# A feed-forward product from seven block products instead of eight, in a two-layer streaming encoder

## The chip, the cores and the metric

The kernel runs on one core of one Trainium2 chip, as one program. The metric is the device time of one execution in microseconds (us); 2145.57 us is the median of three runs before the change (2144.13 to 2145.99). The engines are TensorE (PE, with its weight loads as PEld), VectorE (DVE), ScalarE (ACT), GpSimd (POOL) and SyncE (SP), which issues most DMAs. Each works through its own instructions in order and waits on semaphores for the others.

## The reference

Two layers, each a mixer of three kinds of attention and a feed-forward net with a short convolution. 32 sample rows and 512 prompt rows pass together as T = 544 columns. The change lies in the feed-forward net:

```python
def rmsnorm(x, g):
    xf = x.astype(jnp.float32)
    y = xf * lax.rsqrt(jnp.mean(xf * xf, axis=-1, keepdims=True) + EPS)
    return (y * g.astype(jnp.float32)).astype(x.dtype)

def ffn_layer(x, conv_past, w):
    h = rmsnorm(x, w['ffn_norm_g'])
    a, u = jnp.split(h @ w['ffn_w_up'], 2, axis=-1)
    B, S, _ = a.shape
    pad = jnp.zeros((B, CONV_W - 1, D_FF), a.dtype) if conv_past is None else conv_past
    ap = jnp.concatenate([pad, a], axis=1)
    cw = w['ffn_conv_w']
    c = ap[:, 0:S] * cw[0]
    for k in range(1, CONV_W):
        c = c + ap[:, k:k + S] * cw[k]
    c = c + w['ffn_conv_b']
    out = (jax.nn.silu(c) * u) @ w['ffn_w_down']
    return out, ap[:, -(CONV_W - 1):]
```

D_MODEL is 1024 and D_FF 2816, so `h @ ffn_w_up` has 22 column tiles of 128 for `a` and 22 for `u`.

## The kernel before

Everything is kept transposed: a tile has 128 features on the partitions and the 544 rows of x along the free axis, cut into two halves of H2 = 272 for the PSUM banks. Products are made in a split format: each operand is a high part (rounded to fp32r by ACT, line 345) and a low part (the rest, subtracted by DVE, line 355), and `PASSES` multiplies high by high, high by low and low by high, three matmuls for each block of 128 x 128 weights and 272 columns.

Weights come in the order of `plan()`. `Stream.loader` (212) issues one DMA for each column tile into a `ws` buffer; `Stream.splitter` (226) makes its high and low part in two halves of 512 columns, in a `wx` buffer. In the feed-forward stage a pair i is the tile `("a", l, i)` and the tile `("u", l, i)`, each with 8 blocks along the contraction: 2 x 8 x 2 halves x 3 passes = 96 matmuls. The inputs `h` are x times the gain, not yet divided by the root mean square; the factor `rstd` is multiplied in when a bank is read out (861, 862, 866, and `evac`, 568). `norm_tile` (477) makes the `h` tiles after the output product, `norm_rows` (504) makes `rstd` from the sum of squares with two ACT functions, and `rstd` is ready a few us after the first pair has begun on PE.

`up_tasks` (1850) reads `a` out into `ap`, with two old columns before each request group, applies the three-tap convolution on DVE (1874, 1876, 1878: one TENSOR_SCALAR, two SCALAR_TENSOR_TENSOR) and Silu on ACT (1881), multiplies with `u` (1889, 1890) and splits the result into an `act` tile. The order is pairs 0 to 11, then `down_tasks` over the first 11 `act` tiles, pairs 12 to 21, and `down_tasks` over the rest.

The order of instructions on every engine is written by a planner inside the program: `Sched` (113) runs one generator for each piece of work, keeps a due time for each engine with a cost for each operation (line 297: 1.04 ns a column and 75 ns for a DVE sum, 301: 2.4 ns and 270 ns for a POOL sum), takes the piece that is due first, and hands out buffers through `take` and `give` by the counts in `SLOTS` (251). The costs set the order alone; on the chip each engine then follows its list.

Of the kernel before, what the change touches and what calls it, by code (L numbers as in the profile page):

```python
# [10 lines left out]
F32R = mybir.dt.float32r  # L11
# [93 lines left out]
SWG = 18  # L105

# [92 lines left out]
class Stream:  # L199


    RAW = ("kpsb", "vpsb", "kpdf", "vpdf", "ckN", "ckT", "krp", "ukv")
# [23 lines left out]
    def splitter(self):  # L226
        s, K = self.s, self.K
        for key, n in self.plan:
            if key[0] in self.RAW:
                continue  # L230
            yield from s.take("wx")
            yield from s.need(self.raw, key)
            raw = self.raw.pop(key)[0]
            w = K.t(self.pool, [128, 2, 1024], "wx", F32R)
            h = n // 2
            for a in (0, h):
                yield from K.split(w[:, :, a:a + h], raw[:, a:a + h])
            s.give("ws")
            s.put(self.parts, key, w)

# [12 lines left out]
    ws=3, wx=2, h=8, tf=5, tr=2, rstd=1, post=5,  # L253
    u=2, kk=2, vst=2, vn=2, pk=2, b8=2, p1=1, p2=1, p3=2, p4=2, w1=4, w2=2, wk=3, oa=2, qbd=2, n2=1, an=1, os=1, nm=12,
    ckv=1, uk=1, uv=2, qp=1, qr=1, tq=1, E=1, Ke=1, Ko=1,
    x=8, ap=2, cc=2, act=18, sgl=4,
# [3 lines left out]
class Kern:  # L260
# [216 lines left out]
    def norm_tile(self, m, x, gcol, l, R, late=0):  # L477

        g = self.gpl[l][:, gcol + m:gcol + m + 1]
        h = yield from self.al(self.P, [128, 2, T], "h", F32R)  # L480
# [60 lines left out]
    def proj(self, key, R, post, lasth=False, both=False, tag=None):  # L541

        def chunk(k):
            if k == 0:
                w = yield from self.ws.get(*key)
                return w.rearrange("p s (k c) -> p s k c", c=128)

        def wait(k):
            if ("seen", k) not in R:
                yield from self.s.need(R, ("h", k))  # L550
                R["seen", k] = True

# [128 lines left out]
    def qkv_tasks(self, b, l, u, R, dst):  # L681
# [30 lines left out]
        def past():  # L712
# [7 lines left out]
        return [self.proj((c + "k", l, u), R, kpost, False, first), self.proj((c + "v", l, u), R, vpost, False, False, tag),  # L720
                self.proj((c + "q", l, u), R, qpost, False, False, tag), past]
# [9 lines left out]
    def gate_tasks(self, l, n, R):  # L731
        def mk(i):
            def post(box):
                z = yield from self.evac(box, R)
                self.store(self.sig[i], z, "gpsimd" if i >= SWG else "sync")
                self.s.give("tf", 1, 2000.0)
            return self.proj(("g", l, i), R, post, i == 23)
        return [mk(i) for i in gate_ids(n)]

    def br_tasks(self, l):  # L740
# [11 lines left out]
        def mk(m, b):  # L752
            def chunk(k):
                if k == 0:
                    w = yield from self.ws.get("br", l, b, m)
                    return w[:, :, :512].rearrange("p s (k c) -> p s k c", c=128)

            def free(k):
                if m == 7:
                    self.s.give("act" if b == 2 else "h")  # L760
                if k == 3:
                    self.s.give("wx")
# [28 lines left out]
            return lambda: self.gemm(post, 4, lambda w, k, a: w[:, a, k], lambda k, y: self.o[4 * b + k][0][:, y], T, chunk,  # L791
# [651 lines left out]
    def ml_prep(self, l, u, M, d):  # L1443

        def q_task(h):
            def chunk(k):
                if k == 0:
                    if h == 0:
                        w = yield from self.ws.get("uq", l, u)
                        d["uq"] = w[:, :, :512].rearrange("p s (h k c) -> p s h k c", h=2, k=2)  # L1450
                        yield from self.s.need(M, "cq")
                    return d["uq"]

            def free(k):
# [21 lines left out]
            return lambda: self.gemm(post, 2, lambda w, k, a: w[:, a, h, k], lambda k, b: M["cq"][0][:, k, b], T, chunk,  # L1476
# [333 lines left out]
    def out_tasks(self, l, xsrc, X, R):  # L1810
# [9 lines left out]
        def mk(m):  # L1820
            def chunk(k):
                if k == 0:
                    if m == 0:
                        self.s.spawn(loads())
                    w = yield from self.ws.get("out", l, m)
                    return w.rearrange("p s (k c) -> p s k c", c=128)

            def free(k):
                if m == 7:
                    self.s.give("act")  # L1830
                if k == 7:
                    self.s.give("wx")

            def post(box):
# [9 lines left out]
                yield from self.norm_tile(m, x, G_FFN, l, R)  # L1844

            return lambda: self.gemm(post, 8, lambda w, k, a: w[:, a, k], lambda k, b: self.m2[k][0][:, b], T, chunk,
# [3 lines left out]
    def up_tasks(self, l, i, R, acts):  # L1850
# [3 lines left out]
        def apost(box):  # L1854
# [18 lines left out]
            n = T + 2  # L1873
            self.dscale(c, ap[:, 0:n], self.gain(G_CW + i), ALU.mult, self.gain(G_CB + i), ALU.add)
            yield
            self.stt(c, ap[:, 1:n + 1], self.gain(G_CW + NI + i), c, ALU.mult, ALU.add)
            yield
            self.stt(c, ap[:, 2:n + 2], self.gain(G_CW + 2 * NI + i), c, ALU.mult, ALU.add)
            self.s.give("ap")
            yield  # L1880
            self.act(c, c, AF.Silu)
            yield
# [15 lines left out]
        return [self.proj(("a", l, i), R, apost, False, i == 0), self.proj(("u", l, i), R, upost, i == NI - 1, i == 0)]  # L1898

    def down_tasks(self, l, hf, acts, X, fin):  # L1900
        def mk(m):
            def chunk(k):
                if k in (0, 6):
                    w = yield from self.ws.get("dn", l, m, hf, k // 6)
                    return w.rearrange("p s (k c) -> p s k c", c=128)

            def free(k):
                if m == 7:
                    self.s.give("act")
                if k in (5, 10):  # L1910
# [13 lines left out]
            return lambda: self.gemm(post, 11, lambda w, k, a: w[:, a, k % 6], lambda k, b: acts[11 * hf + k][0][:, b], T,  # L1924
# [4 lines left out]
    def run(self):  # L1929
        tc, nc, a, s = self.tc, self.nc, self.a, self.s  # L1930
        with tc.tile_pool(name="P", bufs=1) as P, tc.tile_pool(name="ps", bufs=1, space=PSUM) as ps, \
# [32 lines left out]
            for l in range(L):  # L1964
# [30 lines left out]
                with tc.tile_pool(name="F", bufs=1) as F:  # L1995
# [299 lines left out]
```

## Time and profile before

| | |
|---|---|
| median of the runs | 2145.57 us |
| profiled execution, its own time | 2145.45 us |
| its span | 2143.2 us |
| PE busy | 2090.4 us (98%) |
| DVE busy | 1482.8 us (69%) |
| ACT busy | 1145.4 us (53%) |
| POOL busy | 414.4 us (19%) |
| DMA, mean over the span | 111 GB/s |

The busy time of PE is modelled, since matmuls are pipelined; a stretch of matmuls is better read by its length and their count. A DVE row gives the length of one instruction, but the next one can begin before it ends, so the cost of one in a full queue is the distance from start to start. In the slices of the page PE is at 9 tenths nearly throughout; DVE stands at 6 to 8 tenths in the attention and in the feed-forward product, and falls to 4 in the down product.

### The profile page before, as it was taken

What the parts mean: (1) busy time and instruction counts of PE and PEld (TensorE: products, weight loads), DVE (VectorE), ACT (ScalarE), POOL (GpSimd) and SP (SyncE); (2) the same over time, 40 slices, a digit from 0 to 9 for tenths busy, and PEclk for the clock granted to TensorE, in tenths of its full rate; (3) what the DMA queues carried; (4) which work ended last, traced back from release to release, by engine and by line L of the source; (5) the groups of instructions that cost most, each with busy time, mean ns of one, the idle gap of its engine ahead of it and who ended that gap; (6) DMA issues with size and microseconds to landing.
All of it is one profiled execution on the core that took longest, in us unless ns stands there. A gap on an engine that the chain in (4) does not pass through costs nothing.

```text
span 2143.2 us, 42022 instructions
## 1 busy us (share of the span) xinstructions
PE 2090.4 (98%) x16334; PEld 2041.5 (95%) x16334; DVE 1482.8 (69%) x3217; ACT 1145.4 (53%) x2545; POOL 414.4 (19%) x810
## 2 busy tenths in 40 slices
PE   7999999899999999999989999998999999999999
PEld 7999999899999999999989999998999999999999
DVE  7878798887676664465468777887876766644652
ACT  7867676877444322223367676767764543222321
POOL 2333232334100000000024342323341000000000
PEclk9999999999999999999999999999999999999999
DMA  5333343322562222332433343433226532223222
GB/s 189 106 111 107 129 135 111 107 70 78 197 196 92 89 86 82 99 89 83 127 113 101 106 126 124 145 100 93 84 69 202 185 100 89 83 82 103 82 85 95
DMA packets 86214, 238.44 MB, mean 111 GB/s; under 512 B 10304, under 2 KB 11200, under 8 KB 86016
## 3 DMA queue, kind: packets, MB, share of 16 engines
q1 hardware_dynamic: 82240, 223.51, 32.7%
q0 software_dynamic: 3776, 12.26, 1.6%
q8 instruction: 128, 2.10, 0.4%
q14 instruction: 70, 0.57, 0.1%
HBM read 201.52 MB, written 34.21 MB: 110 GB/s over the span
## 4 chain that ended last, share of the span: by engine, by line
PE 77%; DVE 8%; ACT 8%; issue 3%; POOL 2%; DMA 2%; SPq 0%; ACTq 0%; POOLq 0%; DVEq 0%
PE z L359 54%; PE g L359 19%; PE pv L359 3%; ACT p L289 2%; PE z L365 1%; ACT w L289 1%; ACT tf L289 1%; ACT wx L289 1%; DMA ws<-wts 1%; DVE wx L296 1%; DVE w L296 1%; DVE b L296 1%; DVE tf L296 1%; ACT kk L289 1%; DVE tr L296 0%
## 5 line engine op out<-in xcount | busy, mean ns | idle before, releaser
L359 PE MATMUL g<-h,wx 128*128 128x272 f32 x4800 | 699.8, 292 | 9.1 <-ACT wx L289 9.0
L359 PE MATMUL z<-h,wx 128*128 128x272 f32 x5184 | 655.1, 288 | 5.0 <-DVE x L296 4.8
L359 PEld LDWEIGHTS z<-h,wx 128*128 128x128 f32 x5184 | 652.2, 189 | 6.4 <-DVE x L296 6.3
L359 PEld LDWEIGHTS g<-h,wx 128*128 128x128 f32 x4800 | 641.9, 190 | 16.7 <-ACT wx L289 9.0
L289 ACT ACTIVATE wx<-ws 128x512 fp32r<-128x512 f32 (+3 forms) x656 | 352.3, 561 | 514.7 <-PE z L359 418.1
L296 DVE TENSOR_TENSOR wx<-ws,wx 128x512 fp32r<-128x512 f32 (+3 forms) x656 | 412.8, 634 | 192.5 <-ACT wx L289 190.0
L359 PE MATMUL z<-act,wx 128*128 128x272 f32 x3264 | 410.7, 288 | 0.0
L359 PEld LDWEIGHTS z<-act,wx 128*128 128x128 f32 x3264 | 410.1, 188 | 0.0
L1870 POOL COPY conv<-ap 128x2 f32<-128x2 f32 x44 | 8.2, 185 | 819.8 <-DVE ap L296 819.8
L289 ACT ACTIVATE w<-z 128x512 fp32r<-128x512 f32 (+9 forms) x212 | 90.1, 441 | 76.2 <-PE pv L359 31.5
L296 DVE TENSOR_TENSOR tf<-g,rstd 128x272 f32<-128x272 f32 x184 | 79.7, 433 | 42.0 <-PE g L359 37.5
L296 DVE TENSOR_TENSOR ap<-z,rstd 128x32 f32<-128x32 f32 x132 | 41.2, 341 | 87.5 <-PE z L359 84.2
L296 DVE TENSOR_TENSOR tf<-z,rstd 128x272 f32<-128x272 f32 x96 | 42.1, 438 | 78.0 <-PE z L359 78.0
L289 ACT ACTIVATE cc<-cc 128x546 f32<-128x546 f32 x44 | 29.1, 662 | 119.0 <-DVE cc L304 119.0
L359 PE MATMUL pv<-w,vst 128*128 128x512 f32 (+3 forms) x352 | 82.4, 323 | 3.3 <-DVE w L296 3.0
L289 ACT ACTIVATE p<-p 128x512 f32<-128x512 f32 (+4 forms) x160 | 71.6, 461 | 1.8
L304 DVE SCALAR_TENSOR_TENSOR cc<-ap,gp,cc 128x546 f32<-128x546 f32 x88 | 69.1, 785 | 1.6
L296 DVE TENSOR_TENSOR x<-z,x 128x272 f32<-128x272 f32 x64 | 28.0, 438 | 60.4 <-PE z L359 60.4
L317 POOL TENSOR_SCALAR tr<-tf 128x544 fp32r<-128x544 f32 (+2 forms) x66 | 47.4, 719 | 113.0 <-ACT tf L289 63.7
L296 DVE TENSOR_TENSOR w<-z,w 128x512 fp32r<-128x512 f32 (+5 forms) x124 | 55.9, 465 | 17.3 <-ACT w L289 17.1
L317 POOL TENSOR_SCALAR kk<-kk 64x1024 fp32r<-64x1024 f32 x32 | 42.8, 1338 | 116.2 <-DVE kk L296 114.2
L359 PE MATMUL z<-tr,cr 128*128 128x272 f32 (+2 forms) x264 | 55.6, 302 | 8.8 <-DVE tr L296 5.5
(238 smaller groups left out, 2775.8 us busy)
## 6 DMA issues: line engine op xcount, KB each, us to landing
ws<-wts SPq DMA_DIRECT2D x246, 512.0 KB, 3.5
ws<-wts SPq DMA_DIRECT2D x56, 256.0 KB, 2.9
ws<-wts SPq DMA_DIRECT2D x36, 384.0 KB, 3.1
sgl<-sig SPq DMA_DIRECT2D x46, 272.0 KB, 3.3
ws<-wts SPq DMA_DIRECT2D x32, 320.0 KB, 2.9
sig<-tf SPq DMA_DIRECT2D x36, 272.0 KB, 2.1
tf<-od POOLq DMA_DIRECT2D x24, 272.0 KB, 4.5
od<-oa SPq DMA_DIRECT2D x16, 272.0 KB, 2.2
```

Source lines behind the costliest of these rows:

```text
L289: self.nc.scalar.activation(out=out, in_=in_, func=func, **kw)
L296: self.nc.vector.tensor_tensor(out=out, in0=in0, in1=in1, op=op)
L304: self.nc.vector.scalar_tensor_tensor(out=out, in0=in0, scalar=scalar, in1=in1, op0=op0, op1=op1)
L317: self.nc.gpsimd.tensor_scalar(out=out, in0=in_, scalar1=s1, scalar2=1.0, op0=ALU.mult, op1=ALU.mult)
L359: self.nc.tensor.matmul(out=out, lhsT=lhsT, rhs=rhs, start=start, stop=stop, skip_group_check=not chk)
L365: self.nc.tensor.transpose(out, in_, self.ident[:p, :p])
L1870: nc.gpsimd.tensor_copy(out=cv[:, 0:2], in_=ap[:, 546:548])
```

## The change

For pairs 3 to 21 (`NP = 3`) of each layer the two products are made together. Take the 256 output columns (tile a, tile u), the contraction of 1024 in two halves of 512, and the 544 columns in two halves of 272. This is a product of two 2 x 2 block matrices, eight block products before; Strassen's scheme in Winograd's form makes it from seven products of sums of blocks. On the weight side `Stream.pair` makes S1 = A21 + A22, S2 = S1 - A11, S3 = A11 - A21 and S4 = A12 - S2 on POOL (A11, A12 are the halves of tile a, A21, A22 those of u), and splits seven operands of 512 columns instead of four. They lie alternately in `wx` (now 4 buffers of half the size) and in the new `wy` (3). On the input side `right` makes the normalised tiles with `rstd` and the sums T1 to T4 once a layer, in `h` and `act` buffers, on DVE and POOL, beside pairs 0 to 2, which stay as they were. `strassen` runs the seven products in three PSUM banks a pair, with the products A22 and S4 of one pair between those of the next; ACT copies one bank's state on its way (`shared`), so that sums of products are formed by starting from it or by a DVE addition. The first convolution tap moves from DVE to ACT (`conv_silu`), and as `rstd` is in the inputs, banks are read out without it. The attention loses one `w1` buffer; `ws` goes from 3 to 4 and `sgl` from 4 to 5.

```diff
     def splitter(self):
...
+            if key[0] in "au" and key[2] >= NP:
+                if key[0] == "u":
+                    yield from self.pair(key[1], key[2])
+                continue
...
+    def pair(self, l, i):
+        s, K = self.s, self.K
+        yield from s.need(self.raw, ("a", l, i), ("u", l, i))
+        a, u = self.raw.pop(("a", l, i))[0], self.raw.pop(("u", l, i))[0]
+        src = dict(A11=a[:, :512], A12=a[:, 512:], A21=u[:, :512], A22=u[:, 512:])
...
+        def sums():
+            for n, x, y, op, use in (("S1", "A21", "A22", ALU.add, "u"), ("S3", "A11", "A21", ALU.subtract, "au"),
+                                     ("S2", "S1", "A11", ALU.subtract, ("S1", "a")),
+                                     ("S4", "A12", "S2", ALU.subtract, ("a", "S2"))):
+                src[n] = (yield from K.al(K.F, [128, T], "sgl"))[:, :512]
+                K.ptt(src[n], src[x], src[y], op)
...
+        for j, n in enumerate(("A11", "S1", "S2", "A12", "S3", "A22", "S4")):
+            tag = ("wx", "wy")[j % 2]
...
-    ws=3, wx=2, h=8, tf=5, tr=2, rstd=1, post=5,
+    ws=4, wx=4, h=8, tf=5, tr=2, rstd=1, post=5,
...
+    def conv_silu(self, ap, c, i):
+        n = T + 2
+        self.act(c, ap[:, 0:n], AF.Identity, bias=self.gain(G_CB + i), scale=self.gain(G_CW + i))
+        yield
+        self.stt(c, ap[:, 1:n + 1], self.gain(G_CW + NI + i), c, ALU.mult, ALU.add)
+        yield
+        self.stt(c, ap[:, 2:n + 2], self.gain(G_CW + 2 * NI + i), c, ALU.mult, ALU.add)
...
+    def right(self, l, X, R, Q):
+        s = self.s
+        yield from s.need(R, "rstd")
...
+        def one(k):
+            n = []
+            for m in (k, k + 4):
+                t = yield from self.al(self.F, [128, T], "sgl")
+                self.stt(t, X[m][0], self.gain(G_FFN + m), r, ALU.mult, ALU.mult)
...
+            s.spawn(parts(n2, "sgl", "h", (("B21", k), ("B22", k))))
+            m = yield from self.tf()
+            self.tt(m[:, a], n1[:, b], n1[:, a], ALU.subtract)
+            yield
+            self.ptt(n1[:, b], n2[:, b], n1[:, b], ALU.subtract)
+            yield
+            s.spawn(parts(n1, "sgl", "h", (("B11", k), ("T3", k))))
+            self.tt(m[:, b], n2[:, b], m[:, a], ALU.subtract)
...
+            self.ptt(four["t", k // 2][:, (a, b)[k % 2]], n2[:, a], m[:, b], ALU.subtract)
...
+    def strassen(self, l, ids, Q, acts, last):
...
+        def shared(D):
+            yield from s.need(D, "A11")
+            B = yield from self.al(self.ps, [128, 512], "z")
+            self.copy(B[:, :H2], D["A"][:, :H2])
...
+            self.tt(z[:, H2:], t[:, H2:], D["E"][:, :H2], ALU.add)
...
+        def first(D, i):
...
+            yield from s.need(D, "S4")
+            self.tt(ap[:, 276:548], D["u2"][0][:, :H2], D["E"][:, :H2], ALU.add)
...
+        def go():
+            prev = None
+            for i in ids:
+                D = {}
+                D["A"] = yield from self.al(self.ps, [128, 512], "g")
+                yield from prod(D, i, "A11", "B11", D["A"], True, False)
+                s.spawn(shared(D))
+                s.spawn(first(D, i))
+                if prev:
+                    yield from rest(*prev, 0)
+                D["E"] = yield from self.al(self.ps, [128, 512], "pv")
+                yield from prod(D, i, "S1", "T1", D["E"], True, False)
+                if prev:
+                    yield from rest(*prev, 1)
+                yield from s.need(D, "B")
+                yield from prod(D, i, "S2", "T2", D["B"][0], False, False)
+                yield from prod(D, i, "A12", "B21", D["A"], False, True)
+                yield from s.need(D, "u2")
+                yield from prod(D, i, "S3", "T3", D["B"][0], False, False)
+                prev = (D, i)
...
-                    for i in range(12):
+                    for i in range(NP):
                         lst += self.up_tasks(l, i, R2, acts)
+                    Q = {}
+                    s.spawn(self.right(l, X, R2, Q))
+                    lst.append(self.strassen(l, range(NP, 12), Q, acts, False))
                     lst += self.down_tasks(l, 0, acts, X, None)
-                    for i in range(12, NI):
-                        lst += self.up_tasks(l, i, R2, acts)
-
+                    lst.append(self.strassen(l, range(12, NI), Q, acts, True))
```

What stands in the lists is shown for DVE and POOL in the first block of layer 0. In the rows `wx` and `wy` are split weights, `ws` weights as loaded, `sgl` a sum made by POOL, `z`, `g` and `pv` PSUM banks and `cc` and `ap` tiles of the convolution. Line numbers of the changed kernel are higher by about 50 to 200 than those of the kernel before.

DVE, one pair in the middle of the block, before:

```order
L296 TENSOR_TENSOR wx_10107<-ws_9936,wx_10107 128x512
L313 TENSOR_SCALAR cc_10116<-ap_10077,gp_65 128x546
L304 SCALAR_TENSOR_TENSOR cc_10116<-ap_10077,gp_65,cc_10116 128x546
L296 TENSOR_TENSOR wx_10107<-ws_9936,wx_10107 128x512
L304 SCALAR_TENSOR_TENSOR cc_10116<-ap_10077,gp_65,cc_10116 128x546
L296 TENSOR_TENSOR tf_10144<-z_10103,rstd_8788 128x272
L296 TENSOR_TENSOR tf_10144<-z_10140,rstd_8788 128x272
L296 TENSOR_TENSOR wx_10174<-ws_10014,wx_10174 128x512
L296 TENSOR_TENSOR tf_10144<-tf_10144,cc_10116 128x32
L296 TENSOR_TENSOR tf_10144<-tf_10144,cc_10116 128x512
L296 TENSOR_TENSOR wx_10174<-ws_10014,wx_10174 128x512
L296 TENSOR_TENSOR act_10197<-tf_10144,act_10197 128x544
```

Four weight parts, a read-out with `rstd`, three convolution steps and the gate with its split are the work of a pair.

DVE, one pair in the middle of the block, now:

```order
L347 TENSOR_TENSOR ap_9953<-tf_9961,pv_9968 128x272
L347 TENSOR_TENSOR wx_10149<-ws_9935,wx_10149 128x512
L355 SCALAR_TENSOR_TENSOR cc_10161<-ap_9953,gp_65,cc_10161 128x546
L347 TENSOR_TENSOR wy_10150<-sgl_10151,wy_10150 128x512
L355 SCALAR_TENSOR_TENSOR cc_10161<-ap_9953,gp_65,cc_10161 128x546
L347 TENSOR_TENSOR wy_10192<-ws_9935,wy_10192 128x512
L347 TENSOR_TENSOR tf_10084<-z_9956,cc_10161 128x32
L347 TENSOR_TENSOR tf_10084<-z_9956,cc_10161 128x240
L347 TENSOR_TENSOR wx_10213<-sgl_10174,wx_10213 128x512
L347 TENSOR_TENSOR tf_10084<-tf_10084,cc_10161 128x272
L347 TENSOR_TENSOR tf_10229<-tf_10105,pv_10113 128x272
L347 TENSOR_TENSOR wx_10172<-sgl_10196,wx_10172 128x512
```

The four weight parts have become seven, of which this piece holds five; three of them read a sum made by POOL. The rows that multiplied with `rstd` are gone, and the first convolution tap as well; the additions that read a `pv` bank are new.

POOL, the same place, before (small copies into and out of `ap`, and nothing else in a pair):

```order
L1859 MEMSET ap_9399 128x2
L1870 COPY conv<-ap_9399 128x2
L1871 COPY conv<-ap_9399 128x2
L1858 COPY ap_9537<-gp_65 128x2
L1859 MEMSET ap_9537 128x2
```

No instruction of POOL there has more than two columns.

POOL, the same place, now:

```order
L2054 COPY conv<-ap_9843 128x2
L2055 COPY conv<-ap_9843 128x2
L351 TENSOR_TENSOR sgl_10029<-ws_9850,ws_9875 128x512
L351 TENSOR_TENSOR sgl_10051<-sgl_10006,ws_9850 128x512
L351 TENSOR_TENSOR sgl_10073<-ws_9850,sgl_10051 128x512
L2041 COPY ap_10092<-gp_65 128x2
L2042 MEMSET ap_10092 128x2
L351 TENSOR_TENSOR sgl_10151<-ws_9987 128x512
```

Four sums of 512 columns stand between the small copies, and the first copy into `conv` waits for DVE's `ap`.

## Rows read from the trace of the kernel before

**Rows 1.** the head of the page: span, busy time of each engine, its share and instructions

```profile
span 2143.2 us, 42022 instructions
PE 2090.4 (98%) x16334; PEld 2041.5 (95%) x16334; DVE 1482.8 (69%) x3217; ACT 1145.4 (53%) x2545; POOL 414.4 (19%) x810
```

**Rows 2.** timeline of PE, feed-forward part (start, length, instructions merged, idle before)

```profile
673.11 6.51 PE L359 MATMUL z<-h,wx 128*128 128x272 f32 x51
...
699.82 118.16 PE L359 MATMUL z<-h,wx 128*128 128x272 f32 x942
884.10 120.39 PE L359 MATMUL z<-h,wx 128*128 128x272 f32 x960
...
1952.78 120.39 PE L359 MATMUL z<-h,wx 128*128 128x272 f32 x960
```

**Rows 3.** busy time by stretch: PE, PEld, DVE, ACT, POOL, then clock, DMA

```profile
700.00:818.00 118.00, 118.00 (x944) 118.00 (x944) 74.11 (x146) 34.82 (x58) 9.62 (x40) 1.00 0.27 84
884.00:1004.00 120.00, 120.00 (x961) 120.00 (x960) 74.98 (x148) 35.41 (x59) 9.42 (x38) 1.00 0.29 87
```

**Rows 4.** timeline of DVE in one pair of column tiles, 740 to 750 us

```profile
740.56 0.69 DVE L296 TENSOR_TENSOR wx<-ws,wx 128x512 fp32r<-128x512 f32 x1 [0.27 <-ACT wx L289]
742.47 0.69 DVE L296 TENSOR_TENSOR wx<-ws,wx 128x512 fp32r<-128x512 f32 x1
743.07 0.78 DVE L304 SCALAR_TENSOR_TENSOR cc<-ap,gp,cc 128x546 f32<-128x546 f32 x1
743.77 0.44 DVE L296 TENSOR_TENSOR tf<-z,rstd 128x272 f32<-128x272 f32 x1
747.19 0.79 DVE L296 TENSOR_TENSOR tf<-tf,cc 128x32 f32<-128x32 f32 x2
748.70 0.73 DVE L296 TENSOR_TENSOR act<-tf,act 128x544 fp32r<-128x544 f32 x1
749.34 0.50 DVE L296 TENSOR_TENSOR ap<-z,rstd 128x32 f32<-128x32 f32 x2
```

**Rows 5.** groups by shape, 700 to 818 us; the last row over the whole span

```profile
L313 DVE TENSOR_SCALAR cc<-ap,gp 128x546 f32<-128x546 f32 x10 | 5.6, 562 | 0.0
L289 ACT ACTIVATE wx<-ws 128x512 fp32r<-128x512 f32 x36 | 20.8, 624 | 41.6 <-PE z L359 41.6
L289 ACT ACTIVATE cc<-cc 128x546 f32<-128x546 f32 x10 | 6.6, 662 | 28.2 <-DVE cc L304 28.2
...
L289 ACT ACTIVATE wk<-g 128x272 f32<-128x272 f32 x48 | 18.6, 392 | 2.5 <-PE g L359 1.8
```

**Rows 6.** timelines of POOL and DVE, three places in the attention stage

```profile
218.37 1.29 POOL L300 TENSOR_TENSOR u<-tf,u 64x512 fp32r<-64x512 f32 x1
219.00 0.44 DVE L296 TENSOR_TENSOR tf<-g,rstd 128x272 f32<-128x272 f32 x1 [2.36 <-PE g L359]
219.35 0.68 DVE L296 TENSOR_TENSOR vst<-z,vst 128x512 fp32r<-128x512 f32 x1
...
250.25 3.37 POOL L300 TENSOR_TENSOR u<-tf,u 64x512 fp32r<-64x512 f32 x3 [0.85 <-ACT u L289]
250.28 1.81 DVE L296 TENSOR_TENSOR wx<-ws,wx 128x512 fp32r<-128x512 f32 x1
...
430.74 1.71 POOL L300 TENSOR_TENSOR wk<-wk,tq 64x544 f32<-64x544 f32 x1 [1.24 <-DVE wk L304]
433.11 1.36 POOL L300 TENSOR_TENSOR wk<-wk,tq 64x544 f32<-64x544 f32 x1 [0.66 <-DVE wk L304]
430.51 0.72 DVE L296 TENSOR_TENSOR tr<-tf,tr 128x544 fp32r<-128x544 f32 x1
```

**Rows 7.** groups by shape over the whole span: two-input POOL instructions

```profile
L300 POOL TENSOR_TENSOR p<-p,p 128x256 f32<-128x256 f32 x16 | 13.6, 852 | 17.6 <-DVE b L296 17.5
L300 POOL TENSOR_TENSOR p<-p,p 128x128 f32<-128x128 f32 x16 | 9.2, 577 | 12.7 <-DVE b L296 9.8 <-DVE n L296 2.9
```

**Rows 8.** timeline of ACT after the last norm tile of layer 0

```profile
683.98 0.66 ACT L289 ACTIVATE rstd<-rstd 128x544 f32<-128x544 f32 x1
```

More of the change, by code (lines that the diff above doesn't have):

```diff
@@ L105 @@
 SWG = 18
+NP = 3
 class Fiber:
@@ L238, in splitter @@
+            w = []
+            h = -(-n // 256) * 128
+            for a in range(0, n, h):
+                yield from s.take("wx")
+                if not a:
+                    yield from s.need(self.raw, key)
+                    raw = self.raw.pop(key)[0]
+                m = min(h, n - a)
+                t = K.t(self.pool, [128, 2, 512], "wx", F32R)[:, :, :m]
+                yield from K.split(t, raw[:, a:a + m])
+                w += [t[:, :, c:c + 128] for c in range(0, m, 128)]
             s.give("ws")
@@ L239, in splitter, with used, one @@
             s.put(self.parts, key, w)
+    def pair(self, l, i):
[3 more added lines that the diff above has]
+        src = dict(A11=a[:, :512], A12=a[:, 512:], A21=u[:, :512], A22=u[:, 512:])
+        left = dict(a=5, u=3, S1=2, S2=2, S3=1, S4=1)
+        box = {}
+        def used(*names):
+            for n in names:
+                left[n] -= 1
+                if not left[n]:
+                    s.give("ws" if n in "au" else "sgl")
+        def sums():
[4 more added lines that the diff above has]
+                K.ptt(src[n], src[x], src[y], op)
+                used(*use)
+                s.put(box, n)
+                yield
+        def one(n, t, tag):
+            if n[0] == "S":
+                yield from s.need(box, n)
+            yield from K.split(t, src[n])
+            used(n if n[0] == "S" else "u" if n == "A22" else "a")
+            s.put(self.parts, (n, l, i), ([t[:, :, c:c + 128] for c in range(0, 512, 128)], tag))
+        for j, n in enumerate(("A11", "S1", "S2", "A12", "S3", "A22", "S4")):
+            tag = ("wx", "wy")[j % 2]
+            yield from s.take(tag)
+            if j == 0:
+                s.spawn(sums())
+            t = K.t(K.F if j % 2 else self.pool, [128, 2, 512], tag, F32R)
+            s.spawn(one(n, t, tag))
@@ L1872, in apost @@
             c = yield from self.al(self.F, [128, T + 2], "cc")
[L1873 to L1882, printed above, removed]
+            yield from self.conv_silu(ap, c, i)
             self.s.put(st, "c", c)
@@ L1896, in upost @@
             self.s.put(acts, i, t)
-        return [self.proj(("a", l, i), R, apost, False, i == 0), self.proj(("u", l, i), R, upost, i == NI - 1, i == 0)]
+        return [self.proj(("a", l, i), R, apost, None, i == 0),
+                self.proj(("u", l, i), R, upost, "act" if i == NP - 1 else None, i == 0)]
+    def conv_silu(self, ap, c, i):
[5 more added lines that the diff above has]
+        self.stt(c, ap[:, 2:n + 2], self.gain(G_CW + 2 * NI + i), c, ALU.mult, ALU.add)
+        self.s.give("ap")
+        yield
+        self.act(c, c, AF.Silu)
+        yield
@@ new lines, in right, with parts @@
+    def right(self, l, X, R, Q):
+        s = self.s
+        yield from s.need(R, "rstd")
+        r = R["rstd"][0]
+        a, b = slice(0, H2), slice(H2, T)
+        four = {}
+        def parts(x, src, tag, names):
+            o = yield from self.al(self.P if tag == "h" else self.F, [128, 2, T], tag, F32R)
+            yield from self.split(o, x)
+            s.give(src)
+            for name, c in zip(names, (a, b)):
+                s.put(Q, name, o[:, :, c])
+        def one(k):
[3 more added lines that the diff above has]
+                self.stt(t, X[m][0], self.gain(G_FFN + m), r, ALU.mult, ALU.mult)
+                n.append(t)
+                yield
+            n1, n2 = n
+            s.spawn(parts(n2, "sgl", "h", (("B21", k), ("B22", k))))
+            m = yield from self.tf()
+            self.tt(m[:, a], n1[:, b], n1[:, a], ALU.subtract)
+            yield
+            self.ptt(n1[:, b], n2[:, b], n1[:, b], ALU.subtract)
+            yield
+            s.spawn(parts(n1, "sgl", "h", (("B11", k), ("T3", k))))
+            self.tt(m[:, b], n2[:, b], m[:, a], ALU.subtract)
+            yield
+            if k % 2 == 0:
+                four["t", k // 2] = yield from self.tf()
+            while ("t", k // 2) not in four:
+                yield WAIT
+            self.ptt(four["t", k // 2][:, (a, b)[k % 2]], n2[:, a], m[:, b], ALU.subtract)
+            yield
+            s.spawn(parts(m, "tf", "act", (("T1", k), ("T2", k))))
+            self.count(four, k // 2)
+            if four["n", k // 2] == 2:
+                s.spawn(parts(four["t", k // 2], "tf", "act", (("T4", k - k % 2), ("T4", k - k % 2 + 1))))
+        yield from self.launch([one(k) for k in range(4)], 2)
```

137 lines of the change are left out of this document (99 added, 38 removed).

## The prediction

> **What bounds the kernel now.** I read the head of the page first: PE is busy 2090.4 of 2143.2 us [rows 1], so whatever is saved has to be saved on PE or lost by making PE wait. Then the timeline of PE: the feed-forward product of layer 0 is one block from 673.11 to 699.82 + 118.16 = 818.0 us (pairs 0 to 11) and, after half of the down product, one from 884.10 for 120.39 us (pairs 12 to 21); none of these rows names a wait, and layer 1 repeats the second block to the hundredth [rows 2]. A pair of column tiles is 96 matmuls, and 960 matmuls take 120.39 us: 125.4 ns each, 12.04 us a pair. The granted clock there is 1.00, its upper level, while DVE is busy for 74 of 118 us, ACT for 35 and POOL for 10 [rows 3]. So PE alone bounds this stage, and DVE is the nearest follower.
>
> **What the change takes off PE.** A pair in the new form is 7 products of 4 x 3 = 12 matmuls of the same 272 columns: 84, or 10.53 us. It applies to 19 pairs in each layer: 2 x 19 x 12 x 0.1254 = 57.2 us. That is the ceiling, and it is reached only if the other engines keep a pace of 10.53 us a pair.
>
> **What it puts on DVE.** By the order of instructions a steady period is 15 DVE rows. Spacings from start to start are read off one pair of before [rows 4]: a low part 128x512 takes 0.60 us (742.47 to 743.07), a convolution step 0.70 (743.07 to 743.77), the 544-wide low part 0.64 (748.70 to 749.34); a 272-wide piece takes 0.35 (219.00 to 219.35 in [rows 6]), the 32- and 240-wide ones together 0.42 (0.50 less an overlap of 0.08). Per pair: 7 x 0.60 + 2 x 0.70 + 0.64 + 0.35 = 6.59 us of work whose two inputs both lie in SBUF, and 2 x 0.35 + 0.42 = 1.12 us with one input in PSUM. Sum 7.71 us, already without the TENSOR_SCALAR of 0.56 us that goes to ACT [rows 5]. Alone this would fit into 10.53.
>
> **What it puts on POOL, and what that does to DVE.** Four sums of 128x512 a pair, both inputs in SBUF. The trace has no such shape. Lower end: the 64x512 form, 1.29 us [rows 6]; upper end: 128x256 at 852 ns and 128x128 at 577 [rows 7] extended by their slope, 852 + 2 x 275 = 1400 ns (these means include waits). I take 1.29, the same width. POOL's own load, under 7 us a pair, hides behind PE. But the two engines exclude each other: a DVE low part issued 0.03 us after a POOL sum took 1.81 us in place of 0.69, so it began its work 1.15 us after the sum did; in the other direction a POOL instruction issued while DVE had 0.49 us left (430.51 + 0.72 - 430.74) took 1.71 us where the same one undisturbed took 1.36. DVE instructions that read PSUM (219.00, 219.35) ran through a POOL sum undisturbed [rows 6]. The Trainium skill, "SBUF — State Buffer", section "Who interferes with whom", has this as a rule: a VectorE instruction with two SBUF inputs and a GpSimd instruction that reads SBUF share one read interface, held for the whole instruction, and the other one blocks fully. It speaks against the change, and the trace agrees (1.12 us lost by one low part).
>
> Where DVE always has a next instruction, each sum costs it about 1.1 us (1.15, less the 0.14 us that POOL needs before it reads, since 0.49 us of DVE held it up by only 0.35, plus the lost overlap of 0.08): 4.4 us a pair. Bounds for the period: from below, every PSUM piece hidden under a sum, 6.59 + 4.4 = 11.0 us; from above, nothing hidden, 7.71 + 4.4, plus three waits on ACT like the 0.27 us one [rows 4], 12.9 us. A sum falls on a PSUM piece in proportion to its share of the period (4.4 of 11.9, so about 0.4 of the 1.12 us), and I add 0.2 for waits on ACT: 7.71 + 4.4 - 0.4 + 0.2 = 11.9 us. So DVE with POOL becomes the bound of a steady pair, at almost the old 12.04 us. ACT: 7 x 0.62, three 0.66 and four or five copies out of PSUM of at most 0.39 [rows 5]: about 8 us, hidden behind DVE. The weight loads on SP's queue keep their bytes and order, at a DMA share of 0.27 [rows 3].
>
> **First block (pairs 0 to 11).** The new inputs need normalised tiles, so nothing of them starts before rstd, 683.98 + 0.66 = 684.65 us [rows 8]. From there to the first `ap<-tf,pv` in DVE's order stand 42.8 us of DVE work by the spacings above (14 steps of 0.70, 17 splits of 0.64, 23 weight parts of 0.60, 19 pieces of 0.35, 3 times 0.42 and a few small ones), 8 POOL sums of 272 columns (1.1 x 272/512 = 0.58 each, 4.7 us) and 9 of 512 (9.9): 57.4. Then 7 periods of 11.9 to the last weight part of pair 11, and 1.7 us for its product: 684.65 + 57.4 + 83.3 + 1.7 = 827 against 818.0 at present [rows 2]. That is 9 us late; I take 8, since the first two weight parts run before rstd. PE alone could have been 9 x 1.51 = 13.6 us early; instead it waits at the first new product from 709 (673.11 + 3 x 12.04) to about 720, and little by little after that.
>
> **Second block (pairs 12 to 21).** DVE is nearly idle in the down product, so the seven weight parts and four sums of pair 12 are made under it, and the last pair's conv and gating come after its last product, under the next down product. What is left between is 66.8 us of DVE rows (63 weight parts, 16 conv steps, 8 splits, 26 pieces of 0.35, 8 times 0.42) and 36 sums of 1.1: 106.4, less 3.5 hidden, plus 1.7 of waits, plus 1.7 for the last product: 106. PE's own floor is 105.3. Against 120.4 [rows 2] that is 14 us saved. The last pair's chain (add, ACT scale, two conv steps, Silu, gate, split: about 8 us with hand-overs) is wanted by the down product after 60 matmuls, 7.5 us: I count 1 us lost.
>
> **The rest.** Finer weight slots, one `w1` buffer fewer and the `act` tiles for the norm inputs reshuffle the attention stages. All PE idle time of the run is 52.8 us and none of it is in the blocks above [rows 1, 2], so a gain is bounded by that, and a loss by few us if the buffer is missed at all; I take 0, with 8 us to either side.
>
> Sum: (+8 - 14 + 1) x 2 = -10 us. The profiled execution took 2145.45 us, its span 2143.2; the median of the runs is 2145.57, the same within 0.01%. Forecast 2135 us. One microsecond of the steady period is worth 17 x 2 = 34 us (8.5 periods in each block), so the forecast hangs on the 11.9; at 12.2 the change is worth nothing.
>
> **Rivals.** (1) The exclusion costs nothing because sums fall into DVE's idle time, and PE bounds the new pairs. For it: at 10.53 us DVE would be idle for 2.8 us a pair, and PSUM pieces pass freely. Against it: 6.59 + 4.4 exceeds 10.53. The first block then starts its new products at about 714 us, when 28.9 us of rows are done, and ends at 714.6 + 94.8 = 809.4 (-8.6); the second saves 15.1 less 1: 2145.45 - 2 x 22.7 = 2100 us. (2) Slower: the four in-order queues (POOL sum, ACT high part, DVE low part, POOL's conv copy that waits for DVE's `ap`) add a few tenths to the period. At 12.7 us: -5 + 17 x 0.8 = +8.6 us a layer, 2145.45 + 17 = 2163 us; it decides from 12.2 on. For it: DVE would be full, and a late sum holds up everything queued behind its low part. Against it: the weight slots give each part several us of lead. (3) The two halves cancel: a period near 12.2, no change.
>
> **Chances and range.** Forecast case (period 11.2 to 12.1) 0.42, rival 1 0.13, rival 2 0.34, rival 3 0.11. The own range of the forecast case is 2115 to 2142; the bounds 11.0 and 12.9 give 2115 and about 2179. The range that leaves out no more than 2 in 10 is 2104 to 2170. A measurement of this kernel tells 0.2% (4.3 us) from no change: faster 0.53, same 0.13, slower 0.34.
>
> **What would show it.** In the changed profile: matmuls down by 456; gaps on PE in the new pairs, released by DVE or ACT weight parts; a period of 11.9 us between two `ap<-tf,pv`; DVE over 90% busy there, with the mean of the 128x512 low parts near 1 us and not 0.69; a PE gap of some 11 us before the first new product; the second block near 107 us. A low-part mean near 0.69 would prove the exclusion term wrong, a period over 12.2 the sign.

## The result and the profile after

The changed kernel takes 2240.18 us (median of 4 runs, 2233.01 to 2240.99) against 2145.78 us: ratio 1.0429, 95% interval 1.0414 to 1.0443. It is 94 us slower; 2135 us and a gain had been forecast. The head of its page, which answers to [rows 1]:

```profile
span 2238.0 us, 42025 instructions
PE 2083.4 (93%) x15878; PEld 2024.8 (90%) x15878; DVE 1687.2 (75%) x3271; ACT 1321.9 (59%) x2921; POOL 674.8 (30%) x978
```

The 456 matmuls are gone, but PE is now idle for 155 us of the span in place of 53. Three of the costliest groups (count | busy, mean ns | idle before, and what ended it) say where to look: DVE's conv steps (0.78 us in [rows 4]) and the low part of a sum that goes into `wy` (0.69 us for a low part there) take about twice as long, and PE waits 67 us ahead of one product, A22 with T4, for a copy that ACT makes.

```profile
L355 DVE SCALAR_TENSOR_TENSOR cc<-ap,gp,cc 128x546 f32<-128x546 f32 x88 | 131.0, 1489 | 4.9 <-ACT cc L340 3.1
L347 DVE TENSOR_TENSOR wy<-sgl,wy 128x512 fp32r<-128x512 f32 x38 | 60.6, 1596 | 0.0
L410 PE MATMUL z<-act,wy 128*128 128x272 f32 x456 | 85.5, 351 | 67.0 <-ACT tf L340 67.0
```

Timeline of PE around the two blocks of layer 0, answering to [rows 2]: block 1 ends at 854.35 (818.0 before), block 2 runs from 920.05 to 1052.92, 132.9 us in place of 120.4. The down product between them is unchanged. The row of ACT answers to [rows 8]: rstd is done at 689.91, 5.3 us later than before.

```profile
854.35 65.87 PE L410 MATMUL z<-act,wx 128*128 128x272 f32 x528
920.05 1.67 PE L410 MATMUL g<-h,wx 128*128 128x272 f32 x12
...
1052.92 7.26 PE L410 MATMUL z<-act,wx 128*128 128x272 f32 x57
```

```profile
689.25 0.66 ACT L340 ACTIVATE rstd<-rstd 128x544 f32<-128x544 f32 x1
```

In the steady part of block 2 the period is 12.9 or 14.4 us by turns, 13.65 on average, and not 11.9. Busy time of two such periods (PE, PEld, DVE, ACT, POOL, clock, DMA), to be set beside [rows 3]. No engine is full in them (DVE, the nearest, stands idle for 1.1 and 2.6 us), so the period must come from a chain of waits.

```profile
962.60:975.40 12.80, 10.69 (x86) 10.47 (x85) 11.69 (x15) 7.10 (x15) 7.15 (x8) 1.00 0.24 69
975.40:989.80 14.40, 12.29 (x87) 12.06 (x86) 11.81 (x15) 7.24 (x15) 7.16 (x8) 0.88 0.25 83
```

**The loop.** It is read by following one period through four timelines. PE (a row is one product of 12 matmuls; `z<-act,wy` is A22, `pv<-act,wy` S1, `pv<-h,wx` S4, `z<-h,wx` S3):

```profile
970.65 1.76 PE L410 MATMUL z<-act,wy 128*128 128x272 f32 x12 [2.11 <-ACT tf L340]
972.25 1.65 PE L410 MATMUL pv<-act,wy 128*128 128x272 f32 x12
973.75 1.65 PE L410 MATMUL pv<-h,wx 128*128 128x272 f32 x12
...
978.24 1.66 PE L410 MATMUL z<-h,wx 128*128 128x272 f32 x12
...
983.53 2.83 PE L410 MATMUL z<-act,wy 128*128 128x272 f32 x12 [2.12 <-ACT tf L340]
986.16 2.17 PE L410 MATMUL pv<-act,wy 128*128 128x272 f32 x12
```

DVE after the S4 product:

```profile
975.44 0.44 DVE L347 TENSOR_TENSOR ap<-tf,pv 128x272 f32<-128x272 f32 x1 [0.73 <-PE pv L410]
...
976.85 1.69 DVE L355 SCALAR_TENSOR_TENSOR cc<-ap,gp,cc 128x546 f32<-128x546 f32 x1
978.46 1.78 DVE L347 TENSOR_TENSOR wy<-sgl,wy 128x512 fp32r<-128x512 f32 x1
980.16 1.82 DVE L355 SCALAR_TENSOR_TENSOR cc<-ap,gp,cc 128x546 f32<-128x546 f32 x1
```

POOL in the same time:

```profile
976.20 1.75 POOL L351 TENSOR_TENSOR sgl<-ws,ws 128x512 f32<-128x512 f32 x1
977.92 1.77 POOL L351 TENSOR_TENSOR sgl<-sgl,ws 128x512 f32<-128x512 f32 x1
979.77 1.63 POOL L351 TENSOR_TENSOR sgl<-ws,sgl 128x512 f32<-128x512 f32 x1
...
982.62 1.27 POOL L351 TENSOR_TENSOR sgl<-ws 128x512 f32<-128x512 f32 x1
```

And ACT: first conv step, then Silu (`cc<-cc`), a weight part, and only then the copy u3 (`tf<-z`):

```profile
975.98 0.84 ACT L340 ACTIVATE cc<-ap,gp 128x546 f32<-128x546 f32 x1
...
982.02 0.66 ACT L340 ACTIVATE cc<-cc 128x546 f32<-128x546 f32 x1 [2.59 <-DVE cc L355]
982.58 0.61 ACT L340 ACTIVATE wx<-sgl 128x512 fp32r<-128x512 f32 x1
983.10 0.38 ACT L340 ACTIVATE tf<-z 128x272 f32<-128x272 f32 x1
```

The copy u3 reads the bank that the S3 product filled at 979.9. It needs nothing of Silu, but Silu of the pair before stands ahead of it in ACT's queue, waiting 2.59 us for the conv steps, and these start from the S4 product, which follows the A22 product that the copy before it released. So A22, S1, S4, `ap`, conv, Silu, copy, A22 is a ring of one period. Three POOL sums lie in it, and three DVE instructions take 1.69, 1.78 and 1.82 us there in place of 0.79, 0.69 and 0.79: 3.0 us. And after every second wait of 2.1 us the granted clock falls: it is 0.57 over the A22 product from 983.53 (1.00 over the one from 970.65), which is mostly the lower of its two levels, 1.2 GHz, and 0.88 over that whole period. The products A22 and S1 then take 2.83 and 2.17 us instead of 1.76 and 1.65.

### The profile page after: what moved, and what is told of

Read it like the earlier page. It is cut to its first block, busy times and chain, and to the rows that moved or that the text cites. A ratio compares the mean times of both kernels' runs of the same rounds, so it can differ in the third digit from the quotient of the medians.

```text
span 2238.0 us, 42025 instructions
## 1 busy us (share of the span) xinstructions
PE 2083.4 (93%) x15878; PEld 2024.8 (90%) x15878; DVE 1687.2 (75%) x3271; ACT 1321.9 (59%) x2921; POOL 674.8 (30%) x978
## 5 line engine op out<-in xcount | busy, mean ns | idle before, releaser
L410 PE MATMUL z<-act,wx 128*128 128x272 f32 x4296 | 552.1, 290 | 12.9 <-DVE wx L347 12.8
L410 PEld LDWEIGHTS z<-act,wx 128*128 128x128 f32 x4296 | 546.0, 191 | 14.6 <-DVE wx L347 14.2
L340 ACT ACTIVATE wx<-ws 128x512 fp32r<-128x512 f32 (+2 forms) x542 | 299.5, 553 | 407.8 <-PE z L410 258.5
L347 DVE TENSOR_TENSOR wx<-ws,wx 128x512 fp32r<-128x512 f32 (+2 forms) x542 | 344.1, 635 | 208.3 <-ACT wx L340 205.5
L410 PE MATMUL z<-h,wx 128*128 128x272 f32 x1416 | 188.3, 291 | 3.1 <-DVE x L347 3.1
L410 PEld LDWEIGHTS z<-h,wx 128*128 128x128 f32 x1416 | 183.1, 192 | 3.8 <-DVE x L347 3.6
L410 PE MATMUL z<-act,wy 128*128 128x272 f32 x456 | 85.5, 351 | 67.0 <-ACT tf L340 67.0
L410 PEld LDWEIGHTS z<-act,wy 128*128 128x128 f32 x456 | 75.8, 239 | 74.6 <-ACT tf L340 74.6
L347 DVE TENSOR_TENSOR wx<-sgl,wx 128x512 fp32r<-128x512 f32 x114 | 100.5, 883 | 3.2 <-ACT wx L340 2.8
L410 PE MATMUL pv<-act,wy 128*128 128x272 f32 x456 | 75.0, 321 | 12.8 <-DVE wy L347 12.8
L410 PE MATMUL pv<-w,vst 128*128 128x256 f32 (+3 forms) x352 | 82.7, 322 | 3.5 <-DVE w L347 2.2
```

Of the source, the lines that this page charges most:

```text
L340: self.nc.scalar.activation(out=out, in_=in_, func=func, **kw)
L347: self.nc.vector.tensor_tensor(out=out, in0=in0, in1=in1, op=op)
L410: self.nc.tensor.matmul(out=out, lhsT=lhsT, rhs=rhs, start=start, stop=stop, skip_group_check=not chk)
```

## The experiments

Theory 1: the order on ACT closes a ring, and the contention between POOL's sums and DVE (each holds up instructions of the other) sets its length; both are needed. Rival 2: the sums simply come late. Rival 3: the order on ACT is the whole of it, contention costs nothing. Four kernels make the corners of a square.

**Sums on DVE** (sums_dve):

```diff
-                K.ptt(src[n], src[x], src[y], op)
+                K.tt(src[n], src[x], src[y], op)
```

> Edit: the four sums and differences of weight halves of each new pair run on DVE instead of POOL; nothing else. Theory 1 (loop with contention): the period of 13.65 us is a loop, PE product with S4, DVE ap, ACT and DVE conv steps, Silu, ACT's copy u3, PE product with A22, and three POOL sums that overlap DVE instructions of the loop add some 3.2 us to it. Without POOL sums the three DVE instructions fall back from 1.7-1.8 us to 0.7-0.8, though two of the four sums, some 0.65 us each, now stand between them: loop about 11.8 us, DVE load 7.7 + 4 x 0.65 = 10.3 us. Period 11.0 to 11.9, total 2240 - 38 x (1.8 to 2.6) = 2140 to 2172 us, mean of the conv's DVE steps back near 0.8 us from 1.49. Rival 3 (only the order on ACT counts, contention costs nothing): DVE gets 2.6 us more work a pair, period 13.7 or more, total 2240 to 2300.

Measured: 2139.46 us, ratio 0.9975 [0.9966, 0.9985], period 10.49 us. PE is busy without a gap at clock 1.00, DVE for 72.59 of 74 us, and the conv steps are back at 0.81 us. (Group rows: count | busy, mean ns.)

```profile
920.00:994.00 74.00, 74.00 (x594) 74.00 (x594) 72.59 (x135) 50.83 (x105) 25.61 (x28) 1.00 0.28 95
```

```profile
L355 DVE SCALAR_TENSOR_TENSOR cc<-ap,gp,cc 128x546 f32<-128x546 f32 x88 | 70.9, 806 | 4.0 <-ACT cc L340 3.8
...
L347 DVE TENSOR_TENSOR sgl<-ws,sgl 128x512 f32<-128x512 f32 x38 | 26.0, 684 | 0.0
```

A little better than theory 1 had it, and this edit turned out not to be one alone: with DVE's times changed, the planner also put the copy u3 ahead of Silu, as ACT's timeline shows. Hence the other corners.

```profile
947.10 0.38 ACT L340 ACTIVATE tf<-z 128x272 f32<-128x272 f32 x1
947.38 0.65 ACT L340 ACTIVATE cc<-cc 128x546 f32<-128x546 f32 x1
```

**Silu after the copies** (silu_late), sums on POOL:

```diff
         self.s.give("ap")
+        self.s.cur.ready += 2500.0
         yield
         self.act(c, c, AF.Silu)
```

> Edit: Silu of a pair is planned 2.5 us later, so that on ACT the copies u2 and u3 of the next pair stand before it; the sums stay on POOL. Theory 1: PE no longer waits for the conv steps (the 2.1 us wait of the A22 product goes, and with it the falls of the granted clock); what bounds next is DVE with its contended instructions, 82.08 of 96 us busy at 7 periods = 11.7 us a period. Period 11.7 to 12.3, total 2240 - 38 x (1.35 to 1.95) = 2166 to 2189 us; conv steps on DVE still near 1.5 us each. Rival 2 (the sums simply come late, the order on ACT does not matter): same period, 2235 to 2245. Rival 3 (order on ACT is the whole loss against the forecast): 11.9 us, about 2174.

Measured: 2178.63 us, ratio 1.0154 [1.0137, 1.0172], period 11.88 us. Rival 2 is out. DVE is now nearly full: busy for 68.97 of 71.2 us.

```profile
928.30:999.50 71.20, 64.89 (x509) 63.56 (x508) 68.97 (x91) 42.85 (x90) 45.08 (x48) 1.00 0.26 87
```

PE's waits for the copies in layer 0 fall from the first row (changed kernel) to the second (us, times, longest), and PE's own busy time over the span, with as many matmuls, from 2083.4 to 2056.3 us:

```profile
PE z L410 <- ACT tf L340: 33.5, 17, 2.1
```

```profile
PE z L410 <- ACT tf L340: 16.1, 17, 1.1
```

Taking both layers alike, 2 x 17.4 us less wait and 27.1 us less slow matmul time are 61.9 us; the spans differ by 60.6. So the clock has 27 of the 61 us. The rows of the changed kernel agree: 18 of its 30 waits of 2.1 us are followed by slow products, which cost 1.5 us each time.

What is left of PE's waits no longer stands ahead of A22. It stands ahead of S3, for the copy u2, which follows the first conv step on ACT, and that step waits for DVE's `ap`:

```profile
964.45 0.84 ACT L340 ACTIVATE cc<-ap,gp 128x546 f32<-128x546 f32 x1 [1.07 <-DVE ap L347]
...
965.71 0.37 ACT L340 ACTIVATE tf<-z 128x272 f32<-128x272 f32 x1
```

```profile
966.14 1.77 PE L410 MATMUL z<-h,wx 128*128 128x272 f32 x12 [1.11 <-ACT tf L340]
```

`ap` is late because DVE has rows ahead of it without a gap. That DVE's load alone would hold the period at 11.9 us is argued from its 97%; no run put the first conv step behind u2.

**Both** (the two edits together):

> Both edits: sums on DVE and Silu after the copies u2 and u3. Theory 1: the loop is open and nothing is contended; DVE load 10.3 us and PE load 10.53 us a period bound, period 10.6 to 11.3, total 2240 - 38 x (2.35 to 3.05) = 2124 to 2151 us. Rival 3: no better than the order on ACT alone with 2.6 us more DVE work, 2174 or more. Rival 2: like the sums on DVE alone.

Measured: 2137.73 us, ratio 0.9968 [0.9956, 0.9980], period 10.56 us: as with the sums on DVE alone, which already have that order.

**Sums on DVE, old order on ACT** (sums_early):

```diff
-                K.ptt(src[n], src[x], src[y], op)
+                K.tt(src[n], src[x], src[y], op)
...
         self.s.give("ap")
+        self.s.cur.ready -= 1000.0
         yield
```

> Edit: the sums on DVE, and Silu planned 1 us earlier, so that on ACT it stands before the next pair's copy u3 again, as in the changed kernel (with the sums on DVE alone the planner had put it behind). It is the fourth corner: old order, no contention. Theory 1 (the loop is as long as its contended instructions make it): chain from ap to the A22 product 0.44 + 0.8 + 2 x 0.8 + two or three DVE instructions of 0.69 between them + Silu 0.66 + two weight parts 1.2 + copy 0.38 = 6.6 to 7.6 us, and the A22, S1 and S4 products 4.5 to 5.0: period 11.1 to 12.4, total 2139 + 38 x (0.6 to 1.9) = 2162 to 2211 us. Rival 3 (order on ACT alone): period 13.65 as in the changed kernel or more, 2235 us or more. Rival (contention alone, the order on ACT costs nothing): 10.5 us, 2136 to 2143 us.

Measured: 2172.07 us, ratio 1.0130 [1.0113, 1.0147], period 11.42 us. The ring is there again, with Silu, two weight parts and the copy one behind the other on ACT, and PE waits, but only 0.66 us, and the clock stays at 1.00:

```profile
962.90 0.43 DVE L347 TENSOR_TENSOR ap<-tf,pv 128x272 f32<-128x272 f32 x1
...
966.50 0.78 DVE L355 SCALAR_TENSOR_TENSOR cc<-ap,gp,cc 128x546 f32<-128x546 f32 x1
```

```profile
967.32 0.66 ACT L340 ACTIVATE cc<-cc 128x546 f32<-128x546 f32 x1 [0.61 <-DVE cc L355]
967.88 1.13 ACT L340 ACTIVATE wx<-sgl 128x512 fp32r<-128x512 f32 x2
968.92 0.38 ACT L340 ACTIVATE tf<-z 128x272 f32<-128x272 f32 x1
```

```profile
969.35 1.77 PE L410 MATMUL z<-act,wy 128*128 128x272 f32 x12 [0.66 <-ACT tf L340]
```

From `ap` to the A22 product it is 6.45 us (962.90 to 969.35) against 8.09 (975.44 to 983.53) in the changed kernel, though two of the four sums now stand in that stretch of DVE. Of the 2.23 us between the mean periods (13.65 and 11.42), about 1.5 are the shorter ring (12.9 us where the clock is up) and about 0.8 the slow products. The square of periods:

| | Silu before u3 | Silu after u3 |
|---|---|---|
| sums on POOL | 13.65 us (2240.2) | 11.88 us (2178.6) |
| sums on DVE | 11.42 us (2172.1) | 10.49 us (2139.5) |

Either edit alone takes 60 to 70 us, both 101. Rivals 2 and 3 are out, and so is contention alone: the old order costs 33 us with no POOL sum in sight. But theory 1's "both are needed" is too strong as well: the POOL sums cost 39 us with Silu behind u3, where there is no such ring and DVE is nearly full. Each of the two has a price of its own, and together they cost 29 us more than the two prices. The corners are not pure, since the planner writes the whole order anew for each edit (in the last one two weight parts stand between Silu and u3, in the changed kernel one).

**Contention by itself** (before_pool): the kernel before, with four POOL sums a pair whose output nobody reads.

```diff
+                for j in range(2):
+                    x = K.t(self.pool, [128, 480], "dum")
+                    K.nc.gpsimd.tensor_tensor(out=x, in0=raw[:, :480], in1=raw[:, 512:992], op=ALU.add)
             s.give("ws")
```

> Edit: the kernel before, with two sums 128x480 of each raw weight tile of the pairs from 3 on written by POOL into a scratch tile that nobody reads (four sums a pair, 38 pairs); no Strassen, nothing waits for them but the release of the raw tile. It prices the contention alone. Theory 1: DVE's two-input instructions that meet a POOL sum take about 1.1 us longer, so the mean of the low weight parts and of the conv steps rises by 0.2 to 0.6 us in the feed-forward blocks and DVE's busy time grows by 38 x (2.5 to 4.5) = 95 to 170 us; the time grows little, 0 to 15 us, since PE is the bound here and has no wait that hangs on one chain through DVE. Rival (contention is no more than a few tenths of a us, and the 1.7 to 1.8 us of the changed kernel come from something else): DVE's busy time within 30 us of before. Rival (any slowing of DVE moves this kernel): 2165 us or more.

Measured: 2142.35 us, ratio 0.9989 [0.9980, 0.9998]: no loss. Yet DVE is busy for 104.42 us in the stretch where [rows 3] have 74.11, and over the span 1605.4 against 1482.8 us: 122.6 us for 152 sums, 0.81 us each.

```profile
700.00:818.00 118.00, 118.00 (x945) 118.00 (x944) 104.42 (x147) 33.91 (x58) 64.43 (x74) 1.00 0.28 84
```

```profile
L308 DVE SCALAR_TENSOR_TENSOR cc<-ap,gp,cc 128x546 f32<-128x546 f32 x20 | 31.9, 1596 | 0.4
L317 DVE TENSOR_SCALAR cc<-ap,gp 128x546 f32<-128x546 f32 x10 | 11.5, 1145 | 0.0
```

So the same contention is free where DVE still keeps up (104 of 118 us) and PE's path does not pass through it in a ring.

**What lies around the new products** (no_strassen, before_w1, ns_w1). The first keeps the finer weight tiles and the other buffers, but makes all 22 pairs by eight products:

```diff
-NP = 3
+NP = 22
...
-                    lst.append(self.strassen(l, range(NP, 12), Q, acts, False))
```

> Edit: all 22 pairs by the old eight block products; the other parts of the change stay (weight tiles in halves with four slots, a fourth load buffer, one w1 buffer fewer, the first conv step on ACT). The profile of the changed kernel has each layer's first feed-forward product begin 6.4 us later than before. If the finer tiles and buffers cause that: before + 2 x 6.4 = about 2158 us. If it comes from elsewhere: 2146 us, no change. In neither case does the first feed-forward product take longer than before (118 to 120 us a block).

Measured: 2154.23 us, ratio 1.0044 [1.0028, 1.0059]. The surroundings cost 9.4 us, in the attention stages. The two others ask which part; before_w1 is the kernel before with one `w1` buffer fewer, ns_w1 is no_strassen with the old counts of three kinds of buffers:

```diff
-    ... w1=4, ...
+    ... w1=3, ...
```

> Edit: the kernel before with three w1 buffers in place of four, nothing else. In the run without Strassen's products the feed-forward part of layer 0 begins 9.2 us later than before, all lost in the attention. If the missing w1 buffer is the cause: 2150 to 2158 us. If not: 2143 to 2147 us.

Measured: 2145.45 us, ratio 1.0005 [0.9996, 1.0014]: not the buffer by itself.

```diff
-    ws=4, ... w1=3, ... sgl=5, wy=3,
+    ws=3, ... w1=4, ... sgl=4,
```

> Edit: no Strassen's products, with four w1 buffers, three load buffers and four sgl buffers as in the kernel before; the weight tiles in halves and the first conv step on ACT stay. If the missing w1 buffer was the cause of the later attention: 2143 to 2148 us. If the weight tiles in halves (and the other order that the planner makes of them) are: 2150 to 2160 us.

Measured: 2148.47 us, ratio 1.0020 [1.0010, 1.0029], just above the first of the two expectations. What stayed, tiles in halves and the first conv step on ACT, explains some 4 us; that the buffer counts in the new plan and not in the old one is likely, but was not shown, since two more slot counts went back with it.

**Four old pairs a layer** (np4), sums on DVE:

```diff
-NP = 3
+NP = 4
```

> Edit: sums on DVE, and four pairs a layer instead of three by the old eight products. In the run with the sums on DVE, PE waits about 12 us and runs some 7 us at a low clock around the first new product of each layer, while DVE prepares right-hand factors and weight parts. Theory: with one more old pair (1.5 us longer than a new one) this preparation is done in time; 8 to 14 us less wait a layer, total 2139 - 2 x (6 to 12) = 2115 to 2127 us. Rival: DVE is full from the arrival of rstd on and the old pair brings its own weight parts, so the wait only moves: 2138 to 2145 us.

Measured: 2124.51 us, ratio 0.9907 [0.9886, 0.9927]: faster than both kernels, and 15 us faster than the sums on DVE with three old pairs, which is the kernel that it differs from by this edit alone. In the changed kernel the first new products wait for weight parts (first fence), and the low clock of the next ones is visible in their length; with the sums on DVE the waits are shorter but still there (second fence). With a fourth old pair three waits in the old pairs remain, but the first new product, at 738.27, has none and runs at full pace (third fence). Around the first new product PE's waits fall from 11.9 to 6.8 us.

```profile
722.56 1.52 PE L410 MATMUL g<-h,wx 128*128 128x272 f32 x10 [0.19 <-DVE wx L347]
...
730.73 2.63 PE L410 MATMUL pv<-act,wy 128*128 128x272 f32 x10 [6.40 <-DVE wy L347]
...
736.94 2.64 PE L410 MATMUL z<-act,wx 128*128 128x272 f32 x10 [3.12 <-DVE wx L347]
```

```profile
728.90 2.64 PE L410 MATMUL pv<-act,wy 128*128 128x272 f32 x10 [3.62 <-DVE wy L347]
...
736.07 2.63 PE L410 MATMUL z<-act,wx 128*128 128x272 f32 x10 [2.43 <-DVE wx L347]
```

```profile
710.53 7.64 PE L410 MATMUL z<-act,wx 128*128 128x272 f32 x48 [3.30 <-DVE wx L347]
719.29 6.27 PE L410 MATMUL z<-act,wx 128*128 128x272 f32 x48 [1.12 <-DVE wx L347]
727.91 10.52 PE L410 MATMUL z<-act,wx 128*128 128x272 f32 x82 [2.36 <-DVE wx L347]
738.27 1.67 PE L410 MATMUL g<-h,wx 128*128 128x272 f32 x12
```

**Four old pairs and both edits** (best2):

> Edit: sums on DVE, Silu after the copies, four old pairs a layer. Both steady periods are at PE's 10.5 us already, so the later Silu should add nothing to the four old pairs with the sums on DVE: 2118 to 2128 us; if the order at the first new pair matters, 2110 to 2118 us.

Measured: 2129.15 us, ratio 0.9928 [0.9912, 0.9945], a little above the bracket; the later Silu adds nothing.

## Why the prediction was wrong

The step that failed is one half sentence: "ACT: ... about 8 us, hidden behind DVE". ACT's load was right (7.10 us busy in a period of 12.8), but a queue is not a load. I asked what each engine has to do in a period, and not what stands in front of what on an engine whose output PE waits for. The copies of `shared` are the first things that ACT makes out of a pair's own products and that PE needs for the next ones, and with Silu ahead of u3 the conv chain of one pair, until then off the path, came between two products.

Point by point:

- **PE's ceiling** (456 matmuls, 10.53 us a period): right; with the sums on DVE the period is 10.49.
- **DVE's load and the exclusion** (11.9 us a period): wrong for the changed kernel, where DVE is not the bound, near for what it described. With Silu behind u3 the period is 11.88 and DVE is busy for 97% of it. That this meets 11.9 so closely is in part luck: there four DVE instructions a period lose 3.7 us together (1.60, 1.78, 1.82 and 1.43 us in place of 0.78, 0.68, 0.78 and 0.68), where 4.4 less 0.4 had been counted, and DVE waits 0.37 us for ACT, where 0.2 had been. POOL's sum, taken as 1.29 us, is 1.27 undisturbed. The 0.81 us a sum in the kernel before are no test of the price, since DVE has idle time there. The forecast rule that one DVE instruction pays for each sum held.
- **First block**: 57.4 us from rstd to the first `ap<-tf,pv` were forecast; it is 59.6 (689.91 to 749.53). PE's gap of 11 us came as 6.40, 3.12 and smaller ones, 13 us with the wait of 3.3 us in the last old pair, but the slow matmuls behind it were not counted. After that the ring: the block ends 164.4 us after rstd, forecast 142.4.
- **Second block**: 106 us forecast, 132.9 measured. With Silu behind u3 it is 116, and with the sums on DVE 106. So ten of the 27 us are a second error, of size: I let DVE's work run from one end of the block to the other. In the kernel with Silu behind u3 DVE has the forecast amount to do, 105.67 us, but is idle for 10.3: 5.0 in the first 25.7 us (one wait of 1.58 and one of 1.96 us for high parts of weights), 2.2 in the steady part, 3.0 in the last 19.1. That the count of weight slots makes those parts late was not tested.

```profile
902.60:1018.57 115.97, 107.39 (x842) 105.41 (x841) 105.67 (x143) 68.29 (x144) 65.45 (x71) 1.00 0.26 85
```

- **The rest at 0, with 8 us to either side**: the surroundings cost 9.4 us without any new product, just outside the margin, and rstd is 5.3 us late in layer 0.
- **Sum**: per layer 5.3 + 22.0 + 26.9 = 54 us over the forecast; the 1 us counted for the last pair's chain did not come (the down product from 1052.92 runs without a wait). Twice 53 is 106, taking both layers alike; the spans differ by 2238.0 - 2132.7 = 105. Figures of the prediction's range were wrong in themselves: by its own 34 us for a microsecond of the period, 12.9 gives 2169 us and not 2179, and 11.2 and 11.0 give 2111 and 2104 and not 2115 for both; none of this reaches 2240.
- **The rivals**: the second had the sign, the in-order queues and the decisive point (12.2 us); it named ACT's weight parts and POOL's conv copy, not the sequence Silu, weight part, u3, and its 12.7 us had neither a ring nor the clock. The signs named in advance came out so: 456 matmuls as said, DVE over 90% busy only in half of the periods (11.69 of 12.80, then 11.81 of 14.40), low parts of sums 0.88 and 1.60 us, a gap at the first new product, but the waits of the steady state released by ACT's copies and not by weight parts.

The rule cited from the Trainium skill ("SBUF — State Buffer", section "Who interferes with whom") is borne out here: the three DVE instructions of the ring take 1.69 to 1.82 us beside POOL sums against 0.68 to 0.81 us with the sums on DVE. Its remark that issue order decides who is blocked also agrees: a POOL sum issued while DVE is at a two-input instruction of this kind (976.20, 977.92, 979.77) takes 1.63 to 1.77 us, and the one issued at 982.62, when DVE is not, takes 1.27.

## What to carry to other kernels

When a change makes the matrix engine wait for a small copy on another engine, write down what stands ahead of that copy in its queue and follow it back; if the trail returns to the matrix engine within one period, the period can't be shorter than that ring, however light the loads. A slow instruction can cost nothing on an engine that still keeps up with the full one, and it lengthens a ring that it lies in: four POOL sums a pair were free in one kernel, cost 39 us where they filled DVE, and 68 us (13.65 against 11.42 us a period) in the ring. Elementwise work that DVE does in 0.69 us is not relieved by POOL at 1.27 us if each sum takes 0.8 us of DVE away.

## What was not expected of the hardware

- A one-input fp32 instruction on DVE, TENSOR_SCALAR 128x546, went from 0.56 us [rows 5] to 1.15 us beside POOL sums, so not only the two-input ones are held up.
- The granted clock fell after every second wait of 2.1 us in the steady part (periods of 12.8 us at 1.00 and 14.4 us at 0.88 by turns), in three of the four blocks after the first two or three in a row, and never in the steady part with waits of 1.1 or 0.66 us a period. Why some and not others is open.
- Four sums on DVE (4 x 0.68 us) cost DVE less than the same four on POOL: DVE's busy time over the span fell from 1687.2 to 1635.2 us though it does 152 instructions more.
